# Eleven stores at the end of the projection stage, issued from ScalarE's queue instead of SyncE's

## The chip, the cores and the metric

The kernel runs on one core of one Trainium2 chip. The metric is the device time of one execution in microseconds (us). Before the change its median over three runs is 2778.39 us.

## The reference

One transformer layer in float32 on 2048 positions of width 1024, with 256 context positions beside them: an adaptive norm, one input projection into seven parts, bidirectional retention (4 heads of 128) beside dense attention (8 query heads on 2 key heads of 64), an output projection, and a feed-forward with squared ReLU. Cut to what matters:

```python
h = _modulate(_rmsnorm(x, norm1_g), sh1, sc1)
rq, rk, rv, rg, aq, ak, av = jnp.split(h @ w_in, SPLIT_IDX, axis=-1)
rq_h = _apply_rope(_heads(rq, RET_HEADS), *ret_cs)           # retention queries
s_f = _retention_final_state(crk_h, crv_h, log_gamma[0])      # from the context
ret, _, _ = _bidir_retention(rq_h, rk_h, _heads(rv, RET_HEADS), log_gamma, s_f, s_b)
ret = _ret_out(ret, rg, ret_gn_g)
att = _latent_attention(q, k, v, kc, vc)
x = x + g1 * (jnp.concatenate([ret, att], axis=-1) @ w_out)   # g1: the gate
x = x + g2 * _sqrelu_mlp(_modulate(_rmsnorm(x, norm2_g), sh2, sc2), w_ff1, w_ff2)
return _rmsnorm(x, final_norm_g)
```

In `_retention_chunkwise` the forward state goes from chunk to chunk: `state = state * c_dec + k^T v`. Every chunk of 128 positions needs the state before it.

## The kernel before

**Three stages in a row.** First the projections (0 to about 630 us), then attention with retention and the output projection beside it (to about 1600 us), then the feed-forward. What the first stage makes for the second goes to DRAM scratch and is read back there: the turned (transposed) queries of retention `qt`, its keys `kt`, rows `rk` and `rv`, gates `rg`, attention's queries `aq`, forward states `sf`, and the output weights times the gate, as a high and a low float16 form, `wod`.

**The end of the first stage.** The last column block is that of the retention queries (`C_RQ`), in 16 rows of 128 positions (row 0 to 15 below). Its work is put into a plan by hand: `at(q, step, fn)` gives each piece a slot `q` and a step, and the program is emitted slot by slot and, within a slot, in the order `dma, mm, turn, copy, work, mix, extra, store`. Each engine and each DMA queue runs its instructions in the order of emission. A row takes two slots:

- `products` (L650 to L652, TensorE) make the row in PSUM, `evacuate` (L657, ScalarE) copies it out as `xs`;
- `rope` (L683 on VectorE, L686 on GpSimd) and `rope_add` (L698, VectorE) make `ys`;
- `turn` (L703, TensorE) transposes it into `psx`, `turned` (L707, ScalarE) copies that to `zs`, a tile with two buffers, and `store_turned` (L710) stores `zs` to `qt`. A later `turned` can write a buffer only when the store out of it has landed.

Beside the rows run `forward_states`, c from 0 to 16 (loads `rkv` L1072, `rkw` L1077 on GpSimd, product `mpr` L1083 on TensorE into one PSUM buffer, `rst` L1092 on VectorE, store to `sf` L1097), and `output_forms`, i from 0 to 7 (load `ow` L969, gate L973 on GpSimd, high form `of` L978 on ScalarE, low form L982 on VectorE, store to `wod` L986). Names below: qt12 is the turned query of row 12, sf12 the state that the step with c = 13 makes, wod7 the last weight form.

**The start of the second stage.** Attention runs in groups of one position tile and one key head. For each group `Group.load` (L160, L161) brings the queries `qr` in four loads, two for each half `e`. Group 1 starts with its score maxima (`piece` L172 on TensorE into `mp`, `maximum` L185 on VectorE into `nm`), while group 0, whose maxima lie in the first stage, is loaded again, its least values (L191) are turned (L196), written into `qr` as rows (L199, L203), and its scores (L209, L210, `st`) and exponentials (L215, L219) begin. Retention's first loads are `ork` and `orv` (L1345).

**DMA issue.** Nearly every transfer is issued from SyncE's queue (SP). An issue waits, in its queue, for the data that it stores or for the buffer that it fills. The framework also gives each DMA one of eight completion counters, DMAHW0 to DMAHW7, in turn; an issue that waits for a counter waits until the transfer that had this counter before it has landed, whichever queue issued that.

Of the kernel before, what the change touches and what calls it, by code (L numbers as in the profile page):

```python
# [27 lines left out]
NT = SEQ // P  # L28
NC = CTX // P
NK = NT + NC  # L30
# [13 lines left out]
C_RQ, C_RK, C_RV, C_RG, C_AQ, C_AKV = 0, 512, 1024, 1536, 2048, 2560  # L44
# [6 lines left out]
def bc(ap, shape):  # L51
    return ap.to_broadcast(shape)
# [3 lines left out]
def layer_kernel(ctx: ExitStack, tc: tile.TileContext, a: dict, out: bass.AP):  # L56
    nc = tc.nc
# [27 lines left out]
    def scratch(name, n, shape, dtype=F32):  # L85
        return [dram.tile(shape, dtype, name=f"{name}{i}", tag=f"{name}{i}") for i in range(n)]
# [8 lines left out]
    sf_d = scratch("sf", NT, [P, 512])  # L95
# [3 lines left out]
    wo_d = dram.tile([P, KT, 2, D], F16, name="wod", tag="wod")  # L99
# [167 lines left out]
    with ExitStack() as st:  # L267
# [26 lines left out]
        def at(q, step, fn, *args):  # L294
            plan.setdefault((q, step), []).append((fn, args))
# [290 lines left out]
        class Row:  # L586
# [120 lines left out]
                nc.scalar.activation(self.z.rearrange("p (h t) -> p h t", h=4), self.pt, AF.Copy)  # L707

            def store_turned(self, dst):
                nc.sync.dma_start(dst[self.i], self.z)  # L710

            def gate(self):
                self.y = op.tile([P, 512], F32, name="ys", tag="ys")
# [203 lines left out]
        def output_forms(q0):  # L917

            x = {}
# [63 lines left out]

            def store(i):
                k, n = i // 2 * 2, i % 2
                nc.sync.dma_start(wo_d[:, k : k + 2, :, n * 512 : (n + 1) * 512], x["f", i])  # L986

            at(q0 - 4, "dma", load)
            at(q0, "extra", greatest)
# [5 lines left out]
            for i in range(KT):  # L995
                q = q0 + 8 + 3 * i
                at(q - 4, "dma", fetch, i)
                at(q, "work", gate, i)
                at(q + 1, "copy", high, i)
                at(q + 1, "extra", low, i)  # L1000
                at(q + 2, "store", store, i)
# [63 lines left out]
        def forward_states(c, q):  # L1065

            x = {}

            def load():
                x["k"] = sg.tile([P, 2, 512], F32, name="rkv", tag="wm")  # L1070
                for i, src in enumerate((rk_d, rv_d)):
                    nc.sync.dma_start(x["k"][:, i], src[c])  # L1072

            def weigh():
                x["w"] = sg.tile([P, 4, P], F32, name="rkw", tag="wmr")
                k = x["k"][:, 0].rearrange("p (h d) -> p h d", h=4)
                nc.gpsimd.tensor_tensor(x["w"], k, bc(kd[:, 0].unsqueeze(2), [P, 4, P]), op=ALU.mult)  # L1077

            def product():
                x["ps"] = psM.tile([P, 4, P], F32, name="mpr", tag="mps", bufs=1)  # L1080
                for h in range(4):
                    v = x["k"][:, 1, h * P : (h + 1) * P]
                    mm(x["ps"][:, h], x["w"][:, h], v, start=True, stop=True)  # L1083

            def update():
                old = states.get("s")
                s = states["s"] = sg.tile([P, 4, P], F32, name="rst", tag="wst", bufs=4)
                if old is None:
                    nc.scalar.activation(s, x["ps"], AF.Copy)
                    return  # L1090
                for h in range(4):
                    nc.vector.scalar_tensor_tensor(  # L1092
                        s[:, h], old[:, h], cd[:, 0, h : h + 1], x["ps"][:, h], op0=ALU.mult, op1=ALU.add
                    )

            def store():
                nc.sync.dma_start(sf_d[c - 1].rearrange("p (h d) -> p h d", h=4), states["s"])  # L1097

            at(q - 5, "dma", load)
            at(q - 2, "mix", weigh)  # L1100
            at(q, "turn", product)
            at(q + 1, "work", update)
            if c > 0:
                at(q + 1, "store", store)
# [26 lines left out]
        states = {}  # L1131
# [863 lines left out]
    with tc.manual_schedule():  # L1995
# [77 lines left out]
        for lo, g0 in ((0, g + 10), (4, g + 14)):  # L2073
# [3 lines left out]
            for m in range(lo, lo + 4):  # L2077
                k = g0 + 1 + m % 4 // 2
# [9 lines left out]
        for g in range(4, NU * 2 * NS):  # L2088
            b, n = divmod(g, 7)
            s, u = divmod(g, NU)  # L2090
# [20 lines left out]
        s = 2 * NS - 1  # L2111
# [96 lines left out]
```

## Time and profile before

| What | Value |
|---|---|
| median of the three runs | 2778.39 us (2777.96 to 2780.16) |
| profiled execution, its own time | 2773.42 us |
| span of the profile (first to last instruction) | 2771.4 us |
| mean granted TensorE clock | 0.991 |
| busy: TensorE, VectorE, ScalarE, GpSimd | 2649.1, 2098.7, 1600.1, 1424.6 us |
| SyncE's queue (q1) | 274538 packets, 398.57 MB |

The profiled execution is 4.97 us shorter than the median of the runs; its span is 2.02 us shorter than its own time. "SPq" and "ACTq" are the instruction queues of SyncE and ScalarE where they issue DMAs. The bracket behind a row of the timeline is the time that the engine sat idle before the instruction, and what ended it. The granted clock (PEclk) is 1.00 at full speed.

### The profile page before, as it was taken

The page shows a single profiled execution, that of the slowest core. Times are in us where ns is not written, and L with a number is a line of the kernel's source. Part 1 is how long each engine was busy: PE and PEld are TensorE (multiplying, and loading weights), DVE is VectorE, ACT ScalarE, POOL GpSimd, SP SyncE. Part 2 cuts the span into 40 slices and gives each one's busy share as a digit, 9 for nine tenths or more (in the row PEclk, how much of TensorE's full clock was granted, in tenths as well). Part 3 has the DMA queues.
Part 4 walks back from the last instruction along what each step waited for, and adds up shares of the span by engine and source line. Part 5 has one row for each costly group of instructions (what it writes and reads, how often), then busy time and mean ns, then how long its engine had stood idle before and what let it go on. Part 6 is the DMA issues. An engine that isn't in the chain of part 4 may idle for free.

```text
span 2771.4 us, 45239 instructions
## 1 busy us (share of the span) xinstructions
PE 2649.1 (96%) x16896; PEld 1430.2 (52%) x16896; DVE 2098.7 (76%) x3306; ACT 1600.1 (58%) x2736; POOL 1424.6 (51%) x1182
## 2 busy tenths in 40 slices
PE   7999999897999999999999889999999999999997
PEld 2545654454666666666666544444444444444443
DVE  4857677668877777777877587988899956666676
ACT  3633762227877777787777576655554564444342
POOL 2623772364755657676767644455556721111155
PEclk8999999999999999999999999999999999999999
DMA  7478758674111231322222665665657332222223
GB/s 260 138 250 292 230 165 273 157 271 160 47 59 53 67 97 57 98 79 85 87 76 83 243 213 173 199 193 179 199 186 277 126 112 79 84 91 77 84 78 136
DMA packets 275046, 402.51 MB, mean 145 GB/s; under 512 B 107717, under 2 KB 163141, under 8 KB 272522
## 3 DMA queue, kind: packets, MB, share of 16 engines
q1 hardware_dynamic: 274538, 398.57, 44.3%
q8 instruction: 133, 2.18, 0.3%
q10 hardware_dynamic: 288, 1.05, 0.1%
q14 instruction: 87, 0.71, 0.1%
HBM read 294.54 MB, written 105.00 MB: 144 GB/s over the span
## 4 chain that ended last, share of the span: by engine, by line
PE 77%; DVE 11%; DMA 3%; ACT 3%; issue 3%; POOL 2%; SPq 0%; POOLq 0%; DVEq 0%; ACTq 0%
PE pu L1712 6%; PE pu L1714 6%; PE pu L1713 6%; PE pd L1891 6%; PE pd L1889 6%; PE pd L1890 6%; PE pso L650 5%; PE pso L651 5%; PE pso L652 5%; PE o L243 3%; PE mp L172 3%; PE st L209 3%; PE st L210 3%; DVE plo L228 2%; DVE nm L185 2%
## 5 line engine op out<-in xcount | busy, mean ns | idle before, releaser
L185 DVE TENSOR_REDUCE nm<-mp 128x1 f32<-128x512 f32 (+1 forms) x576 | 390.0, 684 | 160.4 <-PE mp L172 132.0
L226 POOL TENSOR_TENSOR plo<-p,phi 128x1024 f16<-128x1024 f32 x160 | 351.9, 2201 | 174.3 <-ACT phi L219 142.7
L215 ACT ACTIVATE p<-st 128x512 f32<-128x512 f32 x576 | 339.2, 599 | 175.6 <-PE st L210 120.4
L1712 PE MATMUL pu<-hf,w1f 128*128 128x512 f16 x896 | 339.6, 379 | 8.0 <-ACT w L1729 3.8
L1714 PE MATMUL pu<-hf,w1f 128*128 128x512 f16 x896 | 339.6, 379 | 0.0
L1713 PE MATMUL pu<-hf,w1f 128*128 128x512 f16 x896 | 339.6, 379 | 0.0
L219 ACT ACTIVATE phi<-p 128x1024 f16<-128x1024 f32 x288 | 304.1, 1056 | 0.0
L651 PE MATMUL pso<-wlo,h 128*128 128x512 f16 (+1 forms) x816 | 296.2, 363 | 2.4 <-DVE wlo L548 2.4
L650 PE MATMUL pso<-whi,h 128*128 128x512 f16 (+1 forms) x816 | 296.6, 363 | 1.0 <-ACT whi L547 1.0
L652 PE MATMUL pso<-whi,h 128*128 128x512 f16 (+1 forms) x816 | 296.3, 363 | 0.0
L242 PE MATMUL o<-wv,plo 128*128 128x65 f16 x2304 | 233.8, 193 | 14.4 <-DVE plo L228 7.4
L228 DVE TENSOR_TENSOR plo<-p,phi 128x512 f16<-128x512 f32 x256 | 235.0, 919 | 15.6 <-ACT phi L219 14.4
L243 PE MATMUL o<-wv,phi 128*128 128x129 f16 x2304 | 241.6, 220 | 0.0
L242 PEld LDWEIGHTS <-plo 128*128 128x128 f16 x2304 | 205.4, 98 | 56.0 <-POOL plo L226 15.6
L1915 DVE SCALAR_TENSOR_TENSOR acc<-pd,scv,acc 128x512 f32<-128x512 f32 x248 | 182.9, 742 | 53.2 <-PE pd L1891 50.6
L209 PE MATMUL st<-qr,ks 128*128 128x512 f16 x576 | 219.1, 380 | 4.2 <-ACT p L215 3.8
L210 PE MATMUL st<-qr,ks 128*128 128x512 f16 x576 | 219.0, 380 | 0.1
L172 PE MATMUL mp<-ks,qr 128*128 128x512 f16 x512 | 195.5, 382 | 21.7 <-DVE nm L185 16.4
L243 PEld LDWEIGHTS <-phi 128*128 128x128 f16 x2304 | 204.4, 97 | 21.0
L1677 POOL TENSOR_TENSOR w1s<-w1r 128x512 f32<-128x512 f32 x64 | 91.9, 1436 | 234.1 <-ACT w L1751 160.2
L1889 PE MATMUL pd<-w2t,us 128*128 128x512 f16 x496 | 188.0, 379 | 1.8 <-DVE acc L1915 1.8
L1890 PE MATMUL pd<-w2t,us 128*128 128x512 f16 x496 | 188.0, 379 | 0.0
(377 smaller groups left out, 6101.3 us busy)
## 6 DMA issues: line engine op xcount, KB each, us to landing
w2t<-w2f SPq DMA_DIRECT2D x98, 512.0 KB, 4.1
wm<-in_w_ff SPq DMA_DIRECT2D x64, 512.0 KB, 5.0
w1r<-in_w_ff SPq DMA_DIRECT2D x64, 512.0 KB, 4.7
w2f<-w2f SPq DMA_DIRECT2D x98, 256.0 KB, 2.2
wmr<-in_w_mod SPq DMA_DIRECT2D x32, 512.0 KB, 5.3
w2r<-in_w_ff SPq DMA_DIRECT2D x32, 512.0 KB, 4.5
hf<-hp SPq DMA_DIRECT2D x56, 256.0 KB, 3.6
hf<-hf SPq DMA_DIRECT2D x14, 1024.0 KB, 7.2
```

What stands on the lines that cost most here:

```text
L185: nc.vector.tensor_reduce(dst, src, axis=AX.X, op=ALU.max, negate=True)
L226: nc.gpsimd.tensor_tensor(lo, p, hi, op=ALU.subtract)
L242: mm(o[:, : HD + 1], lo[:, i, c], v[:, : HD + 1], start=False, stop=False)
L243: mm(o, hi[:, i, c], v[:, :VW], start=False, stop=last)
L650: mm(self.ps[:, c], hi[:, k], wh, start=k == 0, stop=False)
L651: mm(self.ps[:, c], hi[:, k], wl, start=False, stop=False)
L652: mm(self.ps[:, c], lo[:, k], wh, start=False, stop=k == KT - 1)
L1712: mm(pu[c], whi, hi, start=first and k == 0, stop=False, **more)
L1713: mm(pu[c], whi, lo, start=False, stop=False, **more)
L1714: mm(pu[c], wlo, hi, start=False, stop=k == 3, **more)
L1889: mm(ps, uh, wh, start=first and j == 0, stop=False, **more)
L1890: mm(ps, uh, wl, start=False, stop=False, **more)
```

## The change

Three kinds of stores get another queue: `qt` of rows 12 to 15, `wod` for i = 5, 6 and 7, and `sf` for c = 13 to 16, eleven DMAs in all. Each stays at its place in the plan, but it is emitted to ScalarE's queue, where it stands between ScalarE's instructions and waits for its data and its counter in their order.

```diff
             def store_turned(self, dst):
-                nc.sync.dma_start(dst[self.i], self.z)
+                late = self.col == C_RQ and self.i >= NT - 4
+                (nc.scalar if late else nc.sync).dma_start(dst[self.i], self.z)
...
             def store(i):
                 k, n = i // 2 * 2, i % 2
-                nc.sync.dma_start(wo_d[:, k : k + 2, :, n * 512 : (n + 1) * 512], x["f", i])
+                queue = nc.scalar if i > 4 else nc.sync
+                queue.dma_start(wo_d[:, k : k + 2, :, n * 512 : (n + 1) * 512], x["f", i])
...
             def store():
-                nc.sync.dma_start(sf_d[c - 1].rearrange("p (h d) -> p h d", h=4), states["s"])
+                queue = nc.scalar if c >= NK - 5 else nc.sync
+                queue.dma_start(sf_d[c - 1].rearrange("p (h d) -> p h d", h=4), states["s"])
```

In the rows that follow a name's last number is that of its buffer, and the bracket holds what an instruction waits for: a counter of DMAs, or an engine.

SyncE's queue at the change of stages, before (`qr_6861` is group 1's tile, `qr_6867` group 0's):

```order
L665 DMA tb128_6671<-in_ret_cs 128x256 [waits DMAHW6_49,Pool_49]
L710 DMA qt12_147<-zs_6690 128x512 [waits DMAHW7_49,Activation_49]
L986 DMA wod_187<-of_6692 128x4x512 [waits DMAHW0_49,DVE_49]
L1097 DMA sf13_181<-rst_6724 128x512 [waits DMAHW1_49,DVE_49]
L710 DMA qt13_148<-zs_6749 128x512 [waits DMAHW2_49,Activation_49]
L1097 DMA sf14_182<-rst_6770 128x512 [waits DMAHW3_49,DVE_49]
L986 DMA wod_187<-of_6763 128x4x512 [waits DMAHW4_49,DVE_49]
L710 DMA qt14_149<-zs_6783 128x512 [waits DMAHW5_49,Activation_49]
L1097 DMA sf15_183<-rst_6793 128x512 [waits DMAHW6_49,DVE_49]
L710 DMA qt15_150<-zs_6800 128x512 [waits DMAHW7_49,Activation_49]
L160 DMA qr_6861<-aq15_134 64x4x128 [waits DMAHW0_49]
L161 DMA qr_6861<-aq15_134 64x2x128 [waits DMAHW1_49]
```

and with the change:

```order
L1074 DMA rkv_6635<-rv16_101 128x512 [waits DMAHW6_49]
L711 DMA qt11_146<-zs_6628 128x512 [waits DMAHW7_49,Activation_49]
L665 DMA tb128_6671<-in_ret_cs 128x256 [waits DMAHW0_49,DVE_49,Pool_49]
L160 DMA qr_6861<-aq15_134 64x4x128 [waits DMAHW7_49]
L161 DMA qr_6861<-aq15_134 64x2x128 [waits DMAHW1_49]
L160 DMA qr_6861<-aq15_134 64x4x128 [waits DMAHW2_49]
L161 DMA qr_6861<-aq15_134 64x2x128 [waits DMAHW3_49]
L160 DMA qr_6867<-aq15_134 64x4x128 [waits DMAHW4_49]
L161 DMA qr_6867<-aq15_134 64x2x128 [waits DMAHW5_49]
L160 DMA qr_6867<-aq15_134 64x4x128 [waits DMAHW6_49]
L161 DMA qr_6867<-aq15_134 64x2x128 [waits DMAHW7_49]
L1348 DMA ork_6890<-rk1_68 128x512 [waits DMAHW0_49,PE_49]
```

The nine stores between the table load `tb128` of row 15 and group 1's first load are gone from this queue. The eight `qr` loads stand right behind the table load, each with the counter of an earlier transfer: the first with that of qt11, and then sf13, qt13, sf14, wod7, qt14, sf15 and, for the eighth, the first `qr` load. Retention's `ork` has the counter of qt15.

ScalarE, from row 12's copy on, before:

```order
L707 ACTIVATE zs_6690<-psx_6651 128x512 [waits DMAHW5_49,PE_49,Activation_49]
L978 ACTIVATE of_6692<-ow_6491 128x2x512 [waits DVE_49,Pool_49]
L657 ACTIVATE xs_6717<-pso_6638,wm8_5335 128x512 [waits DVE_49,PE_49]
L707 ACTIVATE zs_6749<-psx_6712 128x512 [waits DMAHW4_49,PE_49,Activation_49]
L657 ACTIVATE xs_6761<-pso_6699,wm8_5335 128x512 [waits DVE_49,PE_49]
L978 ACTIVATE of_6763<-ow_6609 128x2x512 [waits DVE_49,Pool_49]
L707 ACTIVATE zs_6783<-psx_6756 128x512 [waits DMAHW7_49,PE_49,Activation_49]
L707 ACTIVATE zs_6800<-psx_6788 128x512 [waits DMAHW2_49,PE_49,Activation_49]
L1249 ACTIVATE ks2_6842<-ks_315 64x768 [waits DMAHW1_49]
```

and with the change, from the store of qt12, which follows `xs_6717`, to that of sf15, which stands ahead of the last `zs_6800`:

```order
L711 DMA qt12_147<-zs_6690 128x512 [waits DMAHW3_49,Activation_49]
L988 DMA wod_187<-of_6692 128x4x512 [waits DMAHW4_49,DVE_49]
L1100 DMA sf13_181<-rst_6724 128x512 [waits DMAHW1_49,DVE_49]
L707 ACTIVATE zs_6749<-psx_6712 128x512 [waits DMAHW3_49,PE_49]
L657 ACTIVATE xs_6761<-pso_6699,wm8_5335 128x512 [waits PE_49]
L979 ACTIVATE of_6763<-ow_6609 128x2x512 [waits Pool_49]
L711 DMA qt13_148<-zs_6749 128x512 [waits DMAHW2_49,Activation_49]
L1100 DMA sf14_182<-rst_6770 128x512 [waits DVE_49]
L707 ACTIVATE zs_6783<-psx_6756 128x512 [waits DMAHW7_49,PE_49]
L988 DMA wod_187<-of_6763 128x4x512 [waits DMAHW4_49,DVE_49]
L711 DMA qt14_149<-zs_6783 128x512 [waits DMAHW5_49,Activation_49]
L1100 DMA sf15_183<-rst_6793 128x512 [waits DMAHW6_49,DVE_49]
```

ScalarE's own work keeps its order, with the stores in between. `zs_6749` (row 13) took the buffer of row 11 and waited for the store of qt11 (DMAHW4); now it takes that of row 12 and waits for the store of qt12 (DMAHW3), which is issued ahead of it on the same queue. qt15 follows the first `ks2` copy.

TensorE at the change of stages, with the change; its order is that of before, and the counters are those of the loads named:

```order
L703 MATMUL psx_6788<-ident_60,ys_6785 128x128 [waits DVE_49,Activation_49]
L703 MATMUL psx_6788<-ident_60,ys_6785 128x128 x3
L172 LDWEIGHTS qr_6861 [waits DMAHW7_49,DMAHW1_49]
L172 MATMUL mp_6872<-ks_315,qr_6861 128x512
L196 MATMUL mp_6878<-ident_60,mt0_6849 128x128 [waits DVE_49,Pool_49]
L196 MATMUL mp_6878<-ident_60,mt0_6849 128x128 x3
L172 LDWEIGHTS qr_6861
L172 MATMUL mp_6883<-ks_315,qr_6861 128x512 [waits DVE_49]
L172 LDWEIGHTS qr_6861
L172 MATMUL mp_6886<-ks_315,qr_6861 128x512 [waits DVE_49]
L172 LDWEIGHTS qr_6861
L172 MATMUL mp_6896<-ks_315,qr_6861 128x512 [waits DVE_49]
```

The first `piece` waits for the first two of group 1's four loads alone (DMAHW7 and DMAHW1; before they were DMAHW0 and DMAHW1). Right behind these rows the first score L209 waits for all four loads of group 0 (DMAHW4 to DMAHW7), and the fifth `piece` for the other two of group 1.

## Prediction

> **What bounds the kernel now.** I read the page first, then TensorE's waits, then the chain that ended last around the change of stages, then each queue's timeline there.
>
> ```profile
> PE 2649.1 (96%) x16896; PEld 1430.2 (52%) x16896; DVE 2098.7 (76%) x3306; ACT 1600.1 (58%) x2736; POOL 1424.6 (51%) x1182
> ...
> PE mp L172 <- DMA qr<-aq: 5.0, 1, 5.0
> ```
>
> TensorE is busy for 96% of the span, so a change that touches no matmul can win only where TensorE stands still. Of its waits one is for the transfer that the moved stores precede: group 1's first `piece`, once, 5.0 us. The chain in order of time (start, us, what) shows the way into it:
>
> ```profile
> 629.88 0.64 PE psx L703 x4
> ...
> 630.60 0.61 ACT zs L707
> ...
> 631.22 0.40 SPq L710
> ...
> 631.67 0.62 SPq L160
> ...
> 632.34 3.09 DMA qr<-aq
> ...
> 635.56 0.59 PE mp L172
> ...
> 640.25 0.43 PE st L209
> ```
>
> TensorE ends its last transposes at 630.52. Then ScalarE copies row 15, SyncE stores it (qt15), and only then may the queries be fetched, though nothing in them depends on that store: `aq` was written long before. The second load lands at 635.43 and TensorE goes on. A second cost hangs on the first, in the stretches (length, busy times of the engines, PEclk, DMA share, GB/s):
>
> ```profile
> 634.00:635.00 1.00, 0.00 (x0) 0.00 (x0) 0.00 (x0) 0.00 (x0) 0.00 (x0) 0.58 0.43 88
> ...
> 640.00:641.00 1.00, 1.00 (x4) 0.41 (x3) 0.97 (x2) 0.00 (x0) 0.92 (x1) 0.50 0.63 149
> ...
> 645.00:646.00 1.00, 1.00 (x10) 0.74 (x9) 0.97 (x2) 1.00 (x3) 0.68 (x1) 1.00 0.97 148
> ```
>
> The clock falls to half during the wait and is full again only by 645. So the first scores run at half clock.
>
> **The change part by part.** SyncE's queue before (start, duration, instruction): qt11, then wod7, qt14, sf15, the last `qr` load and the two `ork` loads:
>
> ```profile
> 619.91 0.38 SPq L710 DMA_DIRECT2D qt<-zs  x1
> ...
> 629.16 0.37 SPq L986 DMA_DIRECT2D wod<-of  x1
> 629.62 0.46 SPq L710 DMA_DIRECT2D qt<-zs  x1
> 630.80 0.32 SPq L1097 DMA_DIRECT2D sf<-rst  x1
> ...
> 636.29 0.62 SPq L161 DMA_DIRECT2D qr<-aq  x1
> 637.01 0.54 SPq L1345 DMA_DIRECT2D ork<-rk  x1
> ...
> 640.68 0.59 SPq L1345 DMA_DIRECT2D ork<-rk  x1
> ```
>
> Removed from it: eleven issues of about 0.4 us each and their waits for data. The eight `qr` loads then stand behind the table load of row 15, but each still waits for the counter of an earlier transfer. So they start one by one as those land: the first with qt11, the second with sf13, the third and fourth with qt13 and sf14, group 0's with wod7, qt14 and sf15. When these have their data is VectorE's matter:
>
> ```profile
> 621.56 1.11 DVE L1092 SCALAR_TENSOR_TENSOR rst<-rst,cd,mpr 128x128 f32<-128x128 f32 x4
> ...
> 627.73 1.40 DVE L982 TENSOR_TENSOR of<-ow,of 128x1024 f16<-128x1024 f32 x1
> ...
> 629.66 1.11 DVE L1092 SCALAR_TENSOR_TENSOR rst<-rst,cd,mpr 128x128 f32<-128x128 f32 x4
> ...
> 631.44 0.56 DVE L1250 CAST ks<-unit 64x768 f16<-64x768 f32 x1
> 636.18 0.69 DVE L185 TENSOR_REDUCE nm<-mp 128x1 f32<-128x512 f32 x1 [4.19 <-PE mp L172]
> ```
>
> and how long from issue to landing, from the sources' rows: qt11; wod7; qt14 and qt15; sf15; all `qr` loads from 600 to 700 us; then the two stores that ScalarE's queue already issues, and the landing of each.
>
> ```profile
> DMA to landing us min/median/max: 4.9/4.9/4.9
> ...
> DMA to landing us min/median/max: 2.8/2.8/2.8
> ...
> DMA to landing us min/median/max: 3.0/3.0/3.0
> ...
> DMA to landing us min/median/max: 2.5/2.5/2.5
> ...
> DMA to landing us min/median/max: 2.1/2.3/3.4
> ...
> L1519 ACTq DMA_DIRECT2D x<-xr x2: 345/346/347, 1568.8 to 1592.8; - x2
> ...
> DMA to landing us min/median/max: 4.8/4.8/4.8
> ...
> DMA to landing us min/median/max: 6.4/6.4/6.4
> ```
>
> *Group 1's loads.* sf13's state is ready at 621.56 + 1.11 = 622.67. Issued then and landing after 4.9 us (qt11, in the same burst; ends 3.0 and 6.4), it is down at 627.6, and the second `qr` load starts. With the 3.09 us of the chain's row it lands at 630.7 (ends 628 and 632.5). TensorE is free at 630.52, so the first piece runs at about 630.7, not 635.56. VectorE's first maximum then stands behind its cast `ks`, which ends at 632.00: from here it is VectorE that is late. It gains 636.18 - 632.00 = 4.2 us.
>
> *Group 0's loads* wait for stores whose data come no sooner than before: the low form ends at 629.13 and the last state at 630.77, which is when wod7 and sf15 were issued on SyncE's queue as well (629.16, 630.80). With the landings measured, wod7 is down at 632.0, qt14 at 632.6, sf15 at 633.3. The four loads, 0.65 us apart in the queue (0.62 issue and a gap), start at 632.0, 632.65, 633.3 and 633.95, the last 2.34 us sooner than its 636.29, and land by 633.95 + 2.3 = 636.25.
>
> *The first score* needs them all, and four pieces ahead of it. A piece is a product, 0.59 us even at half clock, and a maximum of 0.69. From 632.0 on three maxima and three products come one after the other, with a cast beside them: the fourth product is done by 632.0 + 3 x 1.28 = 635.8. So the loads bind: the score starts at 636.25, where it was
>
> ```profile
> 640.04 0.63 PE L209 MATMUL st<-qr,ks 128*128 128x512 f16 x1
> ...
> 646.97 0.61 PE L1359 MATMUL bank<-orv,okw 128*128 128x128 f32 x4
> ...
> 643.64 1.04 POOL L1353 TENSOR_TENSOR okw<-ork,kd 128x512 f32<-128x512 f32 x1 [2.52 <-DMA ork<-rk]
> ```
>
> (the last row is what the second of these waits for). That is **3.8 us**. Ends: 5.0 if the loads do not bind and only VectorE's order does; 1.5 and below by slow landings (rivals).
>
> *What comes after the score.* ScalarE now holds sf15's issue (0.35 us) and its wait ahead of row 15's copy: that copy moves from 630.60 to 631.15, the first `ks2` copy (the row of 0.83 below) to 631.65, and qt15's issue to 632.5. Behind it on ScalarE stands group 0's row copy, which is needed only by the score. qt15 lands at 635.5; the first `ork` load, which has its counter, goes from 637.01 to 635.5, and the second from 640.68 to 639.2, 1.5 us sooner. Then the state product of L1359 at 646.97, whose input `okw` GpSimd had at 644.68, can stand at 643.2. It allows those 3.8 us and hardly more.
>
> *The clock.* With TensorE at work from 630.7 on, no idle stretch like 630.5 to 635.5 is left, so I take it to stay full. Four steps of score and piece took 3 x 0.43 = 1.28 us each; at full clock TensorE needs half of that, but VectorE has a maximum in each (0.69) and some two casts (0.56) in the four, 0.97 a step. That is 4 x 0.31 = 1.2 us; the state product holds part of it back. Between 0 and 1.2 I take **0.5**.
>
> *ScalarE's tail of rows, at nothing.* Row 13's copy (624.88) now waits for qt12 and not qt11; the first row is the end of row 15's products on TensorE:
>
> ```profile
> 624.17 0.38 PE L652 MATMUL pso<-whi,h 128*128 128x512 f16 x1
> ...
> 619.15 0.68 ACT L657 ACTIVATE xs<-pso,wm 128x512 f32<-128x512 f32 x1
> 624.88 0.60 ACT L707 ACTIVATE zs<-psx 128x512 f32<-128x512 f32 x1 [5.05 <-DMA qt<-zs]
> 625.38 0.68 ACT L657 ACTIVATE xs<-pso,wm 128x512 f32<-128x512 f32 x1
> ...
> 631.09 0.83 ACT L1249 ACTIVATE ks<-ks 64x768 f16<-64x768 f16 x1
> ```
>
> qt12 goes out right behind the copy that ends at 619.83, 0.1 us before qt11 on the other queue. With the same 4.9 us it is down at 624.75 and the copy stays at 624.88. Its ends: landing in 3.0 us, the tail is limited by row 15's products (over at 624.55; the copy that follows them stood at 625.38) and gains 0.75; landing in 6.4 us, it is down at 626.25 and everything behind it, sf15 included, slips 1.4. The waits of wod6 and sf13 ahead of it are over by 622.7, inside its own wait of 5.05.
>
> *Sum:* 3.8 + 0.5 = **4.3 us**. From the profiled execution's own 2773.42 us (span 2771.4) that gives 2769.1. The median of the runs is 4.97 us above it; 2778.39 - 4.3 = **2774.1 us**.
>
> The Trainium skill speaks against more than this: "DMA: Bandwidth & Descriptors", section "Issuing engines are not separate DMA queues", says that DMAs from any queue run on the same 16 DMA engines and that another issuer saves only the sequencer's issue time. The first rival prices that. Its "TensorE: Matmul & The Clock Gate", Part 1, has the clock fall after an idle window of about 3.4 us; the fall within the 5.05 us wait agrees, and by that rule it would not fall in the short gaps forecast here.
>
> **The rivals.**
>
> 1. *Only issue time is saved.* The loads' start is held by the landings after all, in such a way that only SyncE's time between sf15 and the first load goes: 631.67 - 630.80 = 0.87 us. 2777.5 us. For it: the counters still tie the loads to the stores. Against it: those for group 1 have all landed before 632.
> 2. *Stores from ScalarE's queue land late*, because they share the DMA engines with the loads. sf15 then needs not 2.5 but 4.8 to 6.4 us, as the two stores of L1519: down at 635.6 to 637.2, the last load 0.65 later and 2.3 to land, the score at 638.6 to 640.1. Gain 1.5 to 0, and the 0.5: about 2777.2 us. For it: those two rows; against it: one of the two had 4.8, so the spread is wide, and sf15 took the 2.5 with wod7, qt14 and qt15 in flight beside it.
> 3. *More is won.* qt12 lands in 3.0 us, the tail comes 0.75 sooner with sf15 and qt15, and the clock gives all of its 1.2: 3.8 + 0.75 + 1.2 = 5.75, 2772.6 us. For it: row 15's products end well before its copy. Against it: the burst in which qt11 took 4.9.
> 4. *Slower.* ScalarE runs in order, so its stores' waits hold its copies. qt12 lands after 6.4 us, the tail slips 1.4, sf15 is issued at 632.2 and lands after 6.4 at 638.6; last load 639.25, score at 641.55, 1.5 us later than now: 2779.9 us. It decides from where slip and landing of sf15 together pass 640.04 - 2.3 - 0.65 - 630.80 = 6.3 us. For it: both queues would be slow at once; against it: qt11 took 4.9 with the whole burst ahead of it in one queue.
>
> **How the numbers follow.** Forecast 0.50; rivals 0.08, 0.14, 0.20 and 0.08. About 0.2% (5.6 us) is what a measurement of this kernel can tell from no change. Past it lie most of rival 3 and a little of the forecast: faster 0.25. Slower by that much takes more than rival 4's price: 0.07 with what I have not seen. Within it 0.68. The range takes in rivals 1 to 3 and the runs' own spread (0.4 below to 1.8 above their median): 2771.8 to 2778.9.
>
> **What would show it.** Right: the wait of `mp` L172 for `qr` falls from 5.0 us to under 1; PEclk stays at 1.00 from 630 to 645; the last of group 0's loads starts near 634, the first score near 636; the stores stand in ScalarE's queue with 2.5 to 5 us to landing; row 13's copy stays near 624.9. Wrong: a wait of the scores for `qr` that takes the place of L172's; zs at L707 waiting more than 6 us for qt12; L1359 waiting for `okw` by more than the head start; or a first score 4 us earlier with an unchanged end.

## The result, and the profile after

The changed kernel has a median of 2776.5 us over 20 runs (2772.08 to 2779.9), the kernel before, run beside it, 2779.16 us (2776.15 to 2782.98). The ratio is 0.9988, with a 95% interval of 0.9983 to 0.9994. That is 3.3 us less (1.7 to 4.7; the two medians differ by 2.7), where 4.3 were forecast.

The two profiled executions do not show this in their spans: 2774.9 us after, 2771.4 before. In the profile after, TensorE ended row 15's products at 629.18 us, where it had ended them at 624.55; TensorE was busy without a break from 604 us to there, and the first moved store was issued at 615.26, so the difference lies ahead of the change. All times below, unless they stand in a row of a profile, are **counted from the end of row 15's products on TensorE** (the last L652). Four milestones follow: the first `piece` of group 1, the first score of group 0, the end of a hole that TensorE has later in every version (a `piece` that waits 2.15 us for a maximum, L172 behind L185), and the copy of group 0's finished output (first L247, on ScalarE, "group 0 done"). The last column is the rest of the span.

| profile | first piece | first score | end of hole | group 0 done | rest of span |
|---|---|---|---|---|---|
| before | 11.01 | 15.49 | 42.12 | 49.18 | 2097.7 |
| before_again | 11.26 | 15.74 | 42.21 | 49.28 | 2099.9 |
| before_third | 11.55 | 16.03 | 42.73 | 49.79 | 2100.0 |
| after | 6.54 | 12.14 | 37.34 | 45.96 | 2099.8 |
| after_again | 7.19 | 12.71 | 37.87 | 46.48 | 2100.5 |

Means of each kernel: the first score comes 3.3 us sooner (15.75 to 12.43), the end of the hole 4.75 (42.35 to 37.60), group 0 done 3.2 (49.42 to 46.22). The rest of the span shows no trend beside its scatter of 2.8 us. The gain therefore lies where the forecast put it, and it agrees with the timed 3.3 us.

**The wait is gone.** TensorE's waits in the profile after, from 5 to 46 us behind the end of the products (what waits, for what: total, times, longest):

```profile
PE mp L172 <- DVE nm L185: 5.9, 6, 2.2
...
PE st L209 <- DMA qr<-aq: 0.2, 1, 0.2
```

No row of L172 for `qr` is left, where 5.0 us stood; the scores wait 0.2 us for it. SyncE's queue after (start, duration; the group 1 loads begin at 629.87, group 0's at 636.96):

```profile
629.87 0.62 SPq L160 DMA_DIRECT2D qr<-aq  x1
631.50 0.60 SPq L161 DMA_DIRECT2D qr<-aq  x1
...
636.96 0.57 SPq L160 DMA_DIRECT2D qr<-aq  x1
...
638.33 0.61 SPq L160 DMA_DIRECT2D qr<-aq  x1
638.99 0.62 SPq L161 DMA_DIRECT2D qr<-aq  x1
```

They start one by one, each as the transfer that had its counter lands. The chain that ended last shows the last of these ties binding the first score:

```profile
632.87 2.00 PE mpr L1085 x8
...
634.90 1.12 DVE rst L1094 x4
...
636.05 2.27 DMA sf<-rst
638.33 0.61 SPq L160
...
638.99 2.20 DMA qr<-aq
...
641.32 0.58 PE st L209
```

sf15 lands after 2.27 us, the seventh load starts at that moment and the eighth behind it, and the score starts when it is down. ScalarE's queue after:

```profile
627.91 0.33 ACTq L1100 DMA_DIRECT2D sf<-rst  x1
628.34 0.60 ACT L707 ACTIVATE zs<-psx 128x512 f32<-128x512 f32 x1 [3.31 <-DVE rst L1094]
```

Row 13's copy (L707 at 628.34) was held by the data of sf13, which stands ahead of it in the queue, not by the landing of qt12. It stands 0.84 us before the end of the products, where it stood 0.33 us behind.

**The clock did fall.** The stretches of the profile after, cut where the granted clock changes (length; busy PE, PEld, DVE, ACT, POOL; PEclk; DMA share; GB/s):

```profile
629.55:632.97 3.42, 1.25 (x10) 0.88 (x9) 2.79 (x7) 1.30 (x2) 3.42 (x5) 1.00 0.50 171
632.97:636.38 3.41, 3.38 (x13) 2.44 (x13) 3.17 (x10) 0.60 (x1) 1.11 (x5) 0.50 0.73 250
636.38:639.80 3.42, 1.39 (x6) 0.68 (x7) 2.83 (x8) 3.27 (x5) 0.00 (x0) 0.99 0.84 277
639.80:643.20 3.40, 2.46 (x6) 0.73 (x6) 2.99 (x5) 0.81 (x2) 0.27 (x1) 0.50 0.68 192
643.20:646.60 3.40, 3.40 (x9) 1.42 (x8) 1.67 (x3) 2.27 (x4) 0.77 (x1) 0.50 0.64 181
663.66:667.08 3.42, 1.27 (x13) 0.63 (x11) 2.95 (x3) 1.71 (x3) 1.66 (x1) 1.00 0.00 0
667.08:670.49 3.41, 3.41 (x21) 1.76 (x19) 1.93 (x3) 1.34 (x3) 2.12 (x1) 0.50 0.02 6
```

Three of the first five stretches run at half clock, 10.2 us together, as long as before (three stretches, 634.15 to 644.39). A further one begins at 667.08, right behind the hole; the profile before has none there:

```profile
664.84:668.25 3.41, 1.58 (x21) 1.10 (x21) 2.91 (x4) 1.58 (x3) 1.10 (x2) 1.00 0.00 0
```

Its price is the time from the end of the hole to group 0 done: 8.6 us in both profiles of the changed kernel, 7.06 in all three of before, so 1.55 us.

### The profile page after: what moved, and what is told of

The parts are those of the page before. It is cut to its first block, busy times and chain, and to the rows that moved or that the text cites. A ratio compares the mean times of both kernels' runs of the same rounds, so it can differ in the third digit from the quotient of the medians.

```text
span 2774.9 us, 45229 instructions
## 1 busy us (share of the span) xinstructions
PE 2657.9 (96%) x16896; PEld 1432.6 (52%) x16896; DVE 2103.3 (76%) x3306; ACT 1600.3 (58%) x2736; POOL 1423.2 (51%) x1182
## 4 chain that ended last, share of the span: by engine, by line
PE 76%; DVE 11%; DMA 4%; issue 3%; ACT 3%; POOL 2%; SPq 0%; POOLq 0%; ACTq 0%; DVEq 0%
PE pd L1894 6%; PE pd L1892 6%; PE pd L1893 6%; PE pu L1715 6%; PE pu L1717 6%; PE pu L1716 6%; PE pso L650 5%; PE pso L651 5%; PE pso L652 5%; PE o L243 3%; PE st L209 3%; PE st L210 3%; PE mp L172 3%; DVE plo L228 2%; DVE nm L185 2%
## 5 line engine op out<-in xcount | busy, mean ns | idle before, releaser
L185 DVE TENSOR_REDUCE nm<-mp 128x1 f32<-128x512 f32 (+1 forms) x576 | 390.3, 685 | 158.6 <-PE mp L172 131.4
L652 PE MATMUL pso<-whi,h 128*128 128x512 f16 (+1 forms) x816 | 296.0, 363 | 0.0
L209 PE MATMUL st<-qr,ks 128*128 128x512 f16 x576 | 219.6, 381 | 4.4 <-ACT p L215 3.8
L172 PE MATMUL mp<-ks,qr 128*128 128x512 f16 x512 | 196.1, 383 | 17.2 <-DVE nm L185 17.0
```

The lines of the kernel that those rows point to most:

```text
L185: nc.vector.tensor_reduce(dst, src, axis=AX.X, op=ALU.max, negate=True)
L652: mm(self.ps[:, c], lo[:, k], wh, start=False, stop=k == KT - 1)
```

## The experiments

The milestones of all versions, in us from the end of row 15's products, with the time at half clock ahead of 28 us and behind it:

| profile | first piece | first score | end of hole | group 0 done | half clock, to 28 | behind 28 | ratio to before (95%) |
|---|---|---|---|---|---|---|---|
| before, three | 11.0 to 11.6 | 15.5 to 16.0 | 42.1 to 42.7 | 49.2 to 49.8 | 10.2, 10.2, 17.1 | 0 | |
| after, two | 6.5, 7.2 | 12.1, 12.7 | 37.3, 37.9 | 46.0, 46.5 | 10.2, 10.2 | 3.4, 3.4 | 0.9988 (0.9983 to 0.9994) |
| one_store_back | 11.58 | 16.08 | 42.91 | 49.97 | 17.1 | 0 | 1.0002 (0.9989 to 1.0014) |
| idle_loads | 11.99 | 16.47 | 43.17 | 50.23 | 13.7 | 0 | 1.0006 (0.9993 to 1.0019) |
| last_four | 7.62 | 13.88 | 38.71 | 45.77 | 13.7 | 0 | 0.9991 (0.9982 to 1.0) |
| kept_queries | 7.63 | 13.10 | 39.78 | 46.84 | 13.7 | 0 | 0.9985 (0.9977 to 0.9994) |
| kept_queries_moved | 6.91 | 12.01 | 37.95 | 46.56 | 6.8 | 3.4 | 0.9999 (0.9976 to 1.0022) |
| clock_filled | 6.48 | 12.61 | 37.04 | 45.64 | 0 | 3.4 | 0.9972 (0.9962 to 0.9982) |
| clock_filled_again | 5.52 | 11.84 | 36.65 | 45.26 | 0 | 3.4 | 0.9979 (0.9970 to 0.9987) |
| kept_filled | 7.08 | 12.20 | 37.82 | 44.89 | 0 | 0 | 0.9981 (0.9972 to 0.9991) |
| kept_moved_filled | 6.69 | 11.80 | 35.60 | 42.66 | 0 | 0 | 0.9981 (0.9970 to 0.9992) |

The timed intervals are 3 to 13 us wide from end to end, and most versions differ from each other by less. By time alone one_store_back could still hold a gain of 3.1 us and idle_loads one of 1.9. So the comparisons below rest on the milestones, mostly of one profile each.

The theory to be tested is the prediction's: the loads of the queries were held in SyncE's queue by stores whose data came late, and what is won is set by the counters that still tie the loads to those stores. The rivals are that only issue time was saved, that stores in ScalarE's queue cost something of their own, and that the clock sets what is won.

### More profiles of the two kernels

No edit: the kernel before twice more, the changed one once more.

> The kernel before, unchanged, to see how much the change of stages varies from execution to execution. In the first profile the last transposes L703 ended 5.96 us after the end of row 15's products, at full clock; in the changed kernel and three of its variants 6.75 to 7.84, at half clock. If that is the clock gate's phase and the landing of the stores, it varies here too, between about 5.5 and 8. If it is the price of stores in ScalarE's queue, it stays at 6.0 here. From the end of L703 to the first score 9.5 us again, to L247 43.2, since the wait for qt15 and the loads is still there.

> The same again: the end of L703 anywhere from 5.5 to 8 us after row 15's products if phase and landings make it; 6.0 if the store's queue does. First score 9.5 us and L247 43.2 us after the end of L703.

> The changed kernel again. Theory: the last qr load starts 0.65 us after the landing of sf15, and the score follows the last load's landing, as in the first profile (sf15 landed at 638.32, seventh load 638.33, score 641.32). From the end of L703 to the score 5.0 to 5.8 us, to L247 39.0 to 39.5.

Single times 2776.02, 2780.41 and 2775.0 us. Within one kernel the milestones agree to 0.7 us, the means of the two kernels differ by 3.2 and more. In after_again the score was bound by the other limit that the forecast named, VectorE's order (its first four pieces), and it came 0.57 us later than in after. So the two limits lie within about 1 us of each other.

The last transposes of the rows end at 5.96, 6.15 and 7.08 us in the kernel before and at 6.75 and 7.40 in the changed one. In the versions below they end at 7.84 in kept_queries, whose stores all stand on SyncE's queue, and at 5.69 in clock_filled_again, whose stores stand on ScalarE's while the clock is full. So a price of the stores in ScalarE's queue does not show.

### One store back on SyncE's queue

```diff
-                late = self.col == C_RQ and self.i >= NT - 4
+                late = self.col == C_RQ and NT - 4 <= self.i < NT - 1
```

> Ten stores on ScalarE's queue; qt15 alone is back on SyncE's, where it stands behind the first qr load and ahead of the other seven. Theory (what stands ahead of the loads in their queue holds them): the second load starts only with qt15's issue, some 1.6 us after the end of L703; seven loads 0.65 us apart then take until 5.5, the first piece starts at 4.5 to 5 us after the end of L703, as before, and the score at 7.9 to 9: most of the 4.0 us gain gone, L247 at 42 to 43 after L703's end. Rival (issue time of SyncE): ten elevenths of the gain remain, score at 5.7, L247 at 39.6.

Only qt15 goes back. The framework put it behind the first `qr` load and ahead of the other seven. The whole gain is gone: 2778.65 us, the first score at 16.08. Its chain of waits:

```profile
637.13 0.60 ACT zs L707
637.75 0.33 SPq L711
...
638.13 2.55 DMA qr<-aq
...
640.73 0.61 PE mp L172
```

Ten of the eleven stores are still off the queue, and their issue time is still saved. It is therefore not the issue time that was won, and the first rival falls: one store that waits for its data holds seven loads that need nothing of it.

### Four small loads that shift the counters

```diff
+    def idle_loads():
+        for i in range(4):
+            t = vp.tile([P, 2], F32, name=f"idle{i}", tag=f"idle{i}")
+            nc.sync.dma_start(t, a["pos"])
...
+        on(4, "dma", idle_loads)
```

> The change, with four loads of 1 KB added ahead of group 1's loads, while SyncE's queue has nothing else to issue. They only move the counters on by four: the first qr load then has wod7's counter, the third sf15's, the fifth qt15's. Theory (counters): the third starts with sf15's landing, about 9.1 us after the end of row 15's products, the fifth with qt15's at about 10.7, the last at 12.7, and the score comes at 15.0 to 15.3 instead of 12.14, L247 at 48.5 to 49.2: nearly the whole gain gone. Rival (order in the queue and issue time are what count): four short issues in an idle queue cost nothing, score at 12.1 to 12.4, L247 at 46.0.

The changed kernel with four transfers of 1 KB ahead of group 1's loads; the stores stay on ScalarE's queue. They move each `qr` load to the counter that four loads later had. The gain is gone here too: 2778.52 us, group 0 done at 50.23. SyncE's queue:

```profile
629.03 4.34 SPq L1293 DMA_DIRECT2D idle<-in_pos  x4
635.16 0.61 SPq L160 DMA_DIRECT2D qr<-aq  x1
635.83 0.62 SPq L161 DMA_DIRECT2D qr<-aq  x1
```

and the chain into the first piece:

```profile
632.79 3.02 DMA qt<-zs
...
635.83 2.82 DMA qr<-aq
...
638.78 0.58 PE mp L172
```

The second `qr` load starts within 0.02 us of the landing of qt14, which another engine's queue had issued. The queue itself was free from 633.37 on. Group 1's loads now hang on the stores on which group 0's hung; the second starts 6 us later than in the changed kernel (9.04 against 2.32 and 2.97), and the first piece stands at 11.99. The score was expected at 15.0 to 15.3, bound by group 0's loads; it came at 16.47, because the first piece was this late and four pieces stand ahead of it. One of the ten runs took 2795.3 us. So the counters set what the move wins, as the theory has it: the place in the queue is needed (one_store_back), and it is not enough.

### The last four stores alone

```diff
-                late = self.col == C_RQ and self.i >= NT - 4
+                late = self.col == C_RQ and self.i >= NT - 2
...
-                queue = nc.scalar if i > 4 else nc.sync
+                queue = nc.scalar if i > 6 else nc.sync
...
-                queue = nc.scalar if c >= NK - 5 else nc.sync
+                queue = nc.scalar if c >= NK - 2 else nc.sync
```

> Only wod7, qt14, sf15 and qt15 are issued from ScalarE's queue, the other seven stores stay on SyncE's. Measured from the end of row 15's products on TensorE: the first score came 15.49 us later in the kernel before and 12.14 in the changed one; the copy of group 0's result (L247) 49.18 and 45.96 later. Theory (the loads start when the stores that had their counters land, sf15's landing being the last that counts): the seven others do nothing; score at 12.0 to 12.3, L247 at 45.7 to 46.2, the whole 3.2 us. Rival (only SyncE's issue time is saved): 4 of 11 of the gain, L247 at 48.0. Rival (the early stores on a second queue slow the loads beside them, which made the tail of rows 0.3 to 0.6 us late): the tail comes back, score at 11.6, L247 at 45.5.

wod7, qt14, sf15 and qt15 move, seven stores stay. 2775.92 us, the first score at 13.88, 1.5 us behind the changed kernel's, group 0 done at 45.77. The loads stand right behind sf14 now:

```profile
630.35 0.32 SPq L1100 DMA_DIRECT2D sf<-rst  x1
630.72 0.62 SPq L160 DMA_DIRECT2D qr<-aq  x1
...
637.80 0.62 SPq L161 DMA_DIRECT2D qr<-aq  x1
```

The group 0 loads end with sf15 again, which here took 3.50 us to land. The expectation (score at 12.0 to 12.3) missed by 1.6 us; group 0 is done as early as expected only because no clock was lost behind the hole, whose end (38.71) is 1.1 us later than in the changed kernel. By time, four stores of eleven cannot be told from all eleven; by the milestones they give the larger part.

### No loads of these queries at the change of stages

```diff
-        first_maxima(0, hp, "h0", 1, aq + 20, [rg + i * 30 // 17 for i in range(NK)])
+        at(rg + 24, "dma", groups[1].load, kp, "qr1", 1)
+        first_maxima(0, kp, "qr0", 1, aq + 20, [rg + i * 30 // 17 for i in range(NK)])
...
-            if n > 0:
+            if n > 1:
                 on(k - 14 if n >= EARLY else k + NK - 6, "dma", g.load)
-            else:
-                on(k + NK, "begin", g.load)
```

> The same kept queries, but all eleven stores stay on SyncE's queue as in the kernel before. Theory: once no load stands behind them, the queue of the stores does not matter: score at 11.3 to 11.8 us after the end of row 15's products, L247 at 45.0 to 45.8, within 0.3 us of the same kernel with the stores moved. Rival (the stores themselves must leave SyncE's queue): retention's first loads still stand behind qt15, so the state product waits for okw and L247 comes at 46.5 or later.

> The change, and beside it group 0's queries are kept from the first stage (not loaded twice) and group 1's are loaded there too, so that neither waits for a store. Theory (the stores' landings hold the loads by their counters): with the loads gone from the place, the fourth product of the pieces binds; score 11.3 to 11.8 us after the end of row 15's products (12.14 in the changed kernel, 15.49 before), L247 at 45.0 to 45.6 (45.96 and 49.18), 0.4 to 1.0 us better than the change. Rival (VectorE's order alone binds, the loads are hidden anyway): as the change, 45.96. Rival (the clock is what counts): follows whether it stays full, down to 44.8.

The queries of groups 0 and 1 are loaded in the first stage and stay in SBUF, once with the stores left on SyncE's queue (kept_queries) and once with them moved. The first gives 2774.31 us, 4.2 us less than before (1.7 to 6.4): taking away the loads wins as much as freeing them. Its chain shows what is late once no load is:

```profile
628.97 2.06 PE mpr L1083 x8
...
631.06 1.12 DVE rst L1092 x4
...
632.56 0.27 DVE mt L191 x2
...
632.85 0.56 DVE ks L1251
...
633.44 0.70 DVE nm L185
...
634.18 0.60 PE mp L172
```

It is the last state of retention (L1083, at half clock) and VectorE's order behind it. The score was expected at 11.3 to 11.8 us in both versions and came at 13.10 and 12.01: with the loads gone, that late state was not in the expectation. Group 0 done at 46.84 is the number of the rival that has retention's loads late, but TensorE has no wait for `okw` there. With the stores moved as well the first score comes 1.1 us sooner; group 0 is done at 46.56, where 45.0 to 45.6 was expected, with 3.4 us at half clock behind the hole. Its median is 2775.55 us; one of its runs took 2809.9 us, and the interval is too wide to say more.

### The clock held up

```diff
+                if self.col == C_RQ and self.i == NT - 2:
+                    for _ in range(2):
+                        nc.tensor.transpose(self.pt[:, h], self.y[:, h * P : (h + 1) * P], ident)
...
+    def fill():
+        t = bank(1, (P, 512))
+        for _ in range(3):
+            mm(t, ks[:, 0, :P], ks[:, 0, :512], start=True, stop=True)
...
+        for i in range(5):
+            on(NK + i, "piece", fill)
```

Row 14's transposes are done three times, and three matmuls go in beside each of group 1's first five pieces; nothing uses them. The same edit is made to the changed kernel, to kept_queries and to kept_queries_moved.

> The changed kernel, with matmuls added on TensorE whose results nothing uses: row 14's transposes are done three times, and three products of 128x512 go in beside each of group 1's first five pieces. They fill the stretch from about 2 to 19 us behind the end of row 15's products, in which the changed kernel's TensorE was mostly idle and its clock fell to half. Times below count from the end of row 15's products on TensorE; in the two profiles of the changed kernel the first score stood at 12.14 and 12.71, and the evacuation that follows group 0's attention at 45.96 and 46.48. Theory A (the clock's fall is what the forecast's 0.5 us missed, and it costs 0.5 to 1.2 us): PEclk stays at 1.00 over the stretch, and group 0's evacuation stands at 44.7 to 45.8; the median 0.5 to 1.2 us below the changed kernel's. Theory B (VectorE and the state product set the pace there, so the clock costs nothing): PEclk 1.00 and the evacuation at 45.9 to 46.5 all the same. Theory C: the added products lie in the way of the pieces, each three 0.25 us at full clock; then it is 0.5 to 1 us later than 46.2. If PEclk falls all the same, the run tells nothing on A or B.

> The kernel before, its stores unmoved, with groups 0 and 1 queries loaded already in the first stage and kept (as in kept_queries, whose evacuation stood at 46.84), and with the same added matmuls as in clock_filled. Theory A (clock): 45.3 to 46.3, and a median 4.5 to 5.5 us below before's. Theory B: 46.6 to 47.1 and about 4 us below before's, as kept_queries was.

> The changed kernel with the kept queries (as in kept_queries_moved, whose evacuation stood at 46.56) and the added matmuls of clock_filled. If moving the stores and keeping the queries remove the same wait, this ends within 0.5 us of clock_filled and kept_filled; if each also removes something of its own, it is 0.5 us or more below both. Theory A (clock) has its evacuation at 44.5 to 46, theory B at 46.2 to 46.8.

> The kernel of clock_filled once more, whose one profile had group 0's evacuation at 45.64 us behind the end of row 15's products (the changed kernel: 45.96 and 46.48), and whose timed ratio of 0.9972 says more (7.8 us) than that stage gives (3.2 us for the moved stores and 0.6 for the clock). If the clock's price is 0.6: the evacuation at 45.2 to 46.0 with PEclk at 1.00, and a ratio near 0.9986. If the added matmuls also win elsewhere: a ratio of 0.998 or below again, and a span from the evacuation to the end below the 2097.7 to 2100.5 us that the profiles of before and of the change have there.

The stretches of clock_filled, two from the change of stages and the two about the hole:

```profile
630.00:638.00 8.00, 5.29 (x28) 3.00 (x29) 7.37 (x20) 4.09 (x6) 1.94 (x6) 1.00 0.70 233
638.00:646.00 8.00, 6.55 (x36) 3.62 (x36) 6.52 (x10) 5.34 (x9) 2.72 (x3) 1.00 0.68 183
661.57:664.98 3.41, 1.27 (x19) 0.99 (x19) 2.91 (x4) 1.54 (x2) 1.10 (x2) 1.00 0.00 0
664.98:668.39 3.41, 3.41 (x23) 2.04 (x21) 1.94 (x3) 2.14 (x3) 1.97 (x1) 0.50 0.20 45
```

The clock stays full to the hole in all four profiles with the edit. The hole then ends 0.75 us sooner than without it (36.85 against 37.60, means of two), in kept_filled 1.96 and in kept_moved_filled 2.35 us sooner. So the edit as a whole wins time, 0.75 us in the changed kernel, as theory A has it, and the added matmuls cost less than they win. That this is the clock alone is not shown there: both profiles of clock_filled have a `plo` row of VectorE of 1.67 or 2.05 us where the changed kernel's takes 0.69 (the next section says why that matters). kept_queries and kept_filled have the same such rows, so their 1.96 us come nearest to the price of the clock.

The timed ratios of the changed kernel with the edit, 0.9972 and 0.9979, are 7.8 and 5.8 us below before, where the milestones give 4.0 (49.42 to the mean of 45.64 and 45.26). The medians differ by 5.4 and 6.0 us. The second interval (3.6 to 8.3 us) takes that in, the first (5.0 to 10.6) does not, and neither version was timed against the changed kernel itself in one set of runs. The rest of the span was 2098.6 and 2099.4 us, no less than elsewhere. What the further 1 to 4 us are, if they are there, stays open. The three filled versions cannot be told apart by time.

kept_filled and kept_moved_filled lost no clock behind the hole, and are done earlier than expected (45.3 to 46.3 and 44.5 to 46); the next section says when that clock is lost. Without that loss of 1.55 us the two profiles of clock_filled would have group 0 done at 44.1 and 43.7, where kept_filled has it at 44.89 and kept_moved_filled at 42.66. By the milestones, then, moving the stores and keeping the queries each win 1 to 2.2 us of their own once the clock is held; these are single profiles, and those of one kernel differ by up to 0.7 us. By the medians (2772.37 and 2772.62, 2774.77, 2772.74 us) that does not show.

## Why the prediction was right, and where not

- **What bounds the kernel, right.** The single wait for `qr` was the cost, and it is gone. one_store_back brings it back with one store.
- **Group 1's loads, right, 0.4 to 1.0 us late.** Counted as above the forecast's first piece is at 6.15; it stood at 6.54 and 7.19, right behind the last transposes and waiting for no load.
- **Group 0's loads, right, 0.4 to 1.05 us late.** The last was forecast for 9.40 and started at 9.81 and 10.45. sf15 took 2.27 us to land, forecast 2.5, where the second and the fourth rival needed 4.8 and more.
- **The first score: right in mechanism, 3.3 us instead of 3.8.** Loads and VectorE's order each bound it once. In the profile after, sf15's state was ready at 6.84 (634.90 + 1.12), forecast 6.22. Its product `mpr` ran at half clock, 2.00 us, where the same products take 0.91 at full clock (the row of 616.17 below), and VectorE stood idle 0.21 us for it. The larger part of the 0.62 us VectorE brought along from its rows ahead: its low form began at 3.52, where it had begun at 3.18. In after_again it is 0.28 us for `mpr`, and the low form began at 4.17. The step on the loads took the state's time from before, and neither the clock nor these rows kept to it.

```profile
616.17 0.91 PE mpr L1085 x8
```
```profile
634.90 1.12 DVE L1094 SCALAR_TENSOR_TENSOR rst<-rst,cd,mpr 128x128 f32<-128x128 f32 x4 [0.21 <-PE mpr L1085]
```

- **ScalarE's tail at nothing: the sum right, the reason wrong.** Row 13's copy came 1.2 us sooner, held by sf13's data and not by qt12. The last transposes still ended at 6.75 and 7.40, where they had ended at 5.96 to 7.08, so nothing was won there.
- **What comes after the score, and "the clock": this is the step that failed.** It read that no idle stretch like 630.5 to 635.5 was left and took the clock to stay full, for 0.5 us more. The stretches show it fall twice on windows in which TensorE had no gap above 1.8 us, for 10.2 us at half clock as before. Behind the score two things happened that no step had, and they cancel: 1.4 us were won up to the hole, and 1.55 lost behind it. Together −0.15 instead of +0.5. The two have different causes, so that they cancel is luck.

The **1.4 us** are VectorE's. From about 20 us on it has hardly a gap, and some of its rows take three to four times their usual time when they meet GpSimd's `plo`. The kernel before, VectorE and then GpSimd:

```profile
645.71 2.15 DVE L1250 CAST ks<-unit 64x768 f16<-64x768 f32 x1
...
650.94 2.35 DVE L228 TENSOR_TENSOR plo<-p,phi 128x512 f16<-128x512 f32 x1
```
```profile
645.32 2.13 POOL L226 TENSOR_TENSOR plo<-p,phi 128x1024 f16<-128x1024 f32 x1 [0.63 <-ACT phi L219]
650.62 2.12 POOL L226 TENSOR_TENSOR plo<-p,phi 128x1024 f16<-128x1024 f32 x1 [3.17 <-ACT phi L219]
```

and after:

```profile
647.36 0.74 DVE L1253 CAST ks<-unit 64x768 f16<-64x768 f32 x1
...
651.81 0.68 DVE L228 TENSOR_TENSOR plo<-p,phi 128x512 f16<-128x512 f32 x1
...
653.64 1.26 DVE L1253 CAST ks<-unit 64x768 f16<-64x768 f32 x1
```
```profile
647.64 2.45 POOL L226 TENSOR_TENSOR plo<-p,phi 128x1024 f16<-128x1024 f32 x1
652.32 2.17 POOL L226 TENSOR_TENSOR plo<-p,phi 128x1024 f16<-128x1024 f32 x1 [2.23 <-ACT phi L219]
```

Both long rows of before end about half a microsecond after the GpSimd row that they overlap. After, these two rows start ahead of GpSimd's and take 0.74 and 0.68 us, 3.1 us less together; a later cast takes 1.26 instead of 0.56. Of the first row's 1.4 us VectorE gives back 1.0, most of it because it comes to that row 0.4 us later behind the score and waits 0.5 us for ScalarE's `phi` after it. So 0.4 and 1.7 are won and 0.7 lost. All three profiles of before and kept_queries have both long rows (2.1 to 2.4 us), both profiles of the change have neither. From the first score to the end of the hole that is 26.5 to 26.7 us against 25.2. one_store_back and idle_loads have both long rows too, and take 26.8 and 26.7 us; last_four has 1.34 and 1.04 us in their place, and takes 24.8. That the overlap is the cause fits all of these, but no run varied it alone. The Trainium skill, "SBUF — State Buffer", section "SBUF: two separate sides", has VectorE, in some of its instructions, and GpSimd share one pair of ports, which the one that starts first holds for its whole instruction while the other waits. These rows agree: before, VectorE's two rows start second and end 0.4 and 0.55 us behind GpSimd's; after, they start first, and GpSimd's take 2.45 and 2.17 us where they took 2.13 and 2.12.

The **1.55 us** lost are the half clock behind the hole. The hole is as long before (2.16 us):

```profile
666.67 0.38 PE L172 MATMUL mp<-ks,qr 128*128 128x512 f16 x1 [2.16 <-DVE nm L185]
```

There the boundary of two windows cuts it in two, and the clock stays. In both profiles of the change it lies in one window, which is busy for 1.27 us of 3.42, and the next is at half clock. Without that loss the stage would have won 4.75 us. A fall needs about 2 us of idle time in one window (59% of 3.41; an estimate from these rows). If the boundaries could lie anywhere, about half of the positions would do that to a hole of 2.15 us, in either kernel.

The profiles speak for more than chance. In all 14 of them TensorE last gets its full clock back, ahead of the change of stages, at a boundary 23.1 to 24.7 us before the end of row 15's products, so the boundaries keep to 1.6 of the 3.41 us. Counted on from there, one lies between 40.2 and 41.7 us, mostly inside the hole of before (from 40.0 to 40.6 on, until 42.1 to 42.7). For the changed kernel's hole (from 35.2 and 35.7 on, until 37.3 and 37.9) they lie at 33.4 to 34.9 and at 36.8 to 38.3, and most of these leave it whole. Of the six profiles whose hole ends between 36.6 and 38.0 us five lost the clock behind it (kept_filled, with a boundary at 36.8, did not); of the eight others none did. So the loss seems to go with where the change puts the hole. No run moved the hole alone, so this is not shown. The timed 1.7 to 4.7 us fit 3.2, and 4.75 lies at their edge.

**The rivals.** "Only issue time" would have given 0.87 us, and falls with one_store_back. "Late stores" and "slower" needed landings that did not come. "More is won" needed a full clock, which the change alone does not keep. The sum, 3.2 us by the milestones and 3.3 by the time, falls short of 4.3 by 0.5 for the score and 0.65 for what comes after it.

Of the two rules cited in the prediction: the Trainium skill's "DMA: Bandwidth & Descriptors", section "Issuing engines are not separate DMA queues", has another issuer save only issue time; the transfer itself did take about as long (sf15 2.27 us against 2.5, and 3.50 in last_four). Yet 3.2 us were won where issue time is worth 0.87, because transfers stood queued behind waits. The Trainium skill's "TensorE: Matmul & The Clock Gate", Part 1, has the clock fall after an idle window. The window's length agrees with these traces (3.41 us); here windows that were busy for 1.25 and 1.39 us were enough.

## What to carry to other kernels

Look in a DMA queue for an issue that waits for data, with loads behind it that need nothing of it: what the move can win is read from the landings of the transfers whose counters those loads wait for, on whatever queue these stand, and it can be lost by an unrelated transfer that shifts the counters. When a long wait of TensorE turns into several short ones, do not count on the clock: add up its busy time in windows of 3.41 us, and price each product near there at half speed. Spans of two single profiles, here apart by more than the effect, must be aligned at the last event upstream of the change before they are compared.

## What the runs showed of the hardware

The granted clock changes only at the edges of windows of 3.41 us, and what decides is how much of the last window TensorE was busy. In the twelve profiles with a change of clock between 2 and 48 us, cut into such windows (156 pairs of neighbours), full clock was lost after a window with a busy share of 0.00 to 0.41 (11 times) and kept after one of 0.43 and more. Half clock was left after 0.82 to 1.00, and kept after 0.85 and less, so there the two touch. The first two stretches of the profile after (1.25 of 3.42 busy, then half clock; 3.38 of 3.41 busy, then full) are examples, and so is the one of before that kept its clock with 1.58 of 3.41. The edges lie at another phase in each execution, but not at any: counted back from the end of row 15's products, the one at which full clock returned lies 23.1 to 24.7 us ahead in all 14 profiles.
